# High and low f16 parts, scaled by powers of two, in the output projection of a hybrid attention block

## The chip, the cores and the metric

The kernel runs on one core of a Trainium2 chip. The metric is the device time of one execution in microseconds (us), and beside it stands a profile of one execution, taken by the hardware profiler. The engines are named as in the profile: PE does matrix products (PEld is its weight load), DVE is the vector engine, ACT the scalar engine, POOL is GpSimd, and SP issues nearly all transfers. Each engine works through its own instructions in order and waits for others by semaphores.

## The reference

One encoder layer on x of 1024 tokens by 1024 channels, all in float32:

```python
h = x @ W_in                                  # split by columns into q, k, v, z of two groups
y_a = neighborhood_attention(q_a, k_a, v_a, rel_bias)   # 8 heads of 64, window 8 x 16 on a 16 x 64 grid
y_b = windowed_gqa_with_sink(rotary(q_b), rotary(k_b), v_b, sink)   # 8 query heads, 2 key/value heads, |i-j| <= 128
mixed = concat([y_a * silu(z_a), y_b * silu(z_b)], axis=-1)         # (1024, 1024)
y = mixed @ W_out                             # (1024, 1024)
x = layer_norm(2 ** 0.25 * x + y, gain, bias)
```

The kernel computes `mixed` transposed, in eight tiles of 128 channels by 1024 tokens. Channel tile e holds two heads: e = 0 to 3 are group a, e = 4 to 7 are group b.

## The kernel before

**Precision.** A float32 product is made of three products of shorter parts: high by high, high by low, and low by high, where high is the value rounded to the short type and low the rest. The input projections use f16 parts. They are scaled by powers of two which are found on chip, so that the parts stay in the range of f16, and later steps take the scale out again (`w_scale`, `w_split`). The output projection uses fp32r parts, a float32 form that PE takes at a shorter precision; the profile prints it as f32. It needs no scale.

**Stages.** A first stage, up to about 62 us, loads x and computes v. Then come the projections of `ORDER` (21 column tiles of 128), six of them alone, and the other 15 as *fill* between the attention steps. The attention stage has 128 units: 64 of group b and then 64 of group a, one of 128 queries each. For unit i PE computes scores into a bank of PSUM (`stage_qk`, two products; there are four such banks, tag "s"), DVE adds the bias and finds the row's bound (L719), ACT takes the exponential (L735) and the high part of the probabilities (L745), DVE takes the low part (L746), and SP sends them through a transposing transfer (L749). Six to nine steps later PE multiplies them by v (`stage_pv`, L774), DVE divides by the sum (L783), and PE turns each finished pair of heads round (L794). DVE then multiplies by the gate z and a factor from `z_col` (L797, L803): this is m = `mixed` transposed, kept in the tile of z.

**What sets the order of the work.** The attention stage is written out by hand. The main loop runs over steps i. At a step, PE gets the scores of unit i and then a share of fill (`pump_to`, after the times in `FILL_AT`). Other work waits in four queues ("act", "dve", "pool", "sp") and is let out by `pop` at fixed places, a few operations a step; `need` forces out what something later depends on. The output projection stands at the end of the fill: `out_head` multiplies the channel tiles e = 4 to 7, which are ready first, for some token tiles while attention still runs. `final` does the rest; there, up to the last token tile, the framework's scheduler orders the instructions of each engine.

**The output projection.** `WO_SEQ` numbers the 16 half tiles of w_out (128 by 512, one e and one half a of the output columns): n = 0 to 7 are e = 4 to 7, first for a = 0 and then for a = 1; n = 8 to 15 are e = 0 to 3. `wo_load` loads one at step `WO_LD[n]`. `wo_split` makes its two parts: it copies to the high part (L860, on ACT or DVE) and subtracts for the low part (L864, DVE where n % 3 is 2, else POOL). n = 0 to 7 are split at the steps of `WO_AT` and n = 8 to 15 in `final`. The loads of n = 14 and 15 wait for the splits of 4 and 5. `m_queue` and `m_split` do the same with m: copies on ACT (L880, L831), subtractions on POOL (L881) and DVE (L832). `out_mms` issues the three products for one token tile t, half a and e (L899). All products of one (t, a) add up in a PSUM bank, and `residual` (L946) adds 2 ** 0.25 times x to it on DVE, which also takes the sums for the layer norm. `norm` and `norm_last` do the rest with ACT, DVE and POOL. x_load fetches the tiles of x again for the residual; six tiles fit, so those of t = 6 and 7 are loaded when 0 and 1 have been stored.

The three products of the output projection:

```python
for i, (lh, rh) in enumerate(((mh[e], woh), (mh[e], wol), (ml[e], woh))):
    nc.tensor.matmul(ps, lh[:, ts], rh[:, cs],
                     start=(e == EO[0] and i == 0), stop=(e == EO[-1] and i == 2))
```

Of the kernel before, what the change touches and what calls it, by code (L numbers as in the profile page):

```python
# [24 lines left out]
PSCALE = 2.0 ** 14  # L25
QSCALE = 2.0 ** -15
# [29 lines left out]
def hybrid_block(ctx, tc, xT, x, wt, wv, wo, bias, sink, gain, lbias, cos, sin, bmask, out):  # L56
# [42 lines left out]
    vscb = const.tile([128, 2], F32, name="vscb")  # L99
# [104 lines left out]
    def w_scale(n):  # L204
        g, v = wg[:, n:n + 1], inv[:, n:n + 1]
        c, m = (2 * n, 2) if n < NPRO else (2 * NPRO, NS)
        ps = bank("t")
        nc.tensor.matmul(ps[:, :m], ones, wm.bitcast(BF16)[:, 2 * c + 1:2 * (c + m):2], start=True, stop=True)
        nc.vector.tensor_reduce(g, ps[:, :m], axis=mybir.AxisListType.X, op=ALU.add if n < NPRO else ALU.max)
        nc.vector.tensor_scalar_max(g, g, 2.0 ** -30)  # L210
        nc.vector.tensor_scalar(g.bitcast(I32), g.bitcast(I32), 0x7F800000, None, op0=ALU.bitwise_and)
        nc.vector.tensor_scalar(wsc[:, n:n + 1].bitcast(I32), g.bitcast(I32), 0x7F800000, None, op0=ALU.bitwise_xor)
# [112 lines left out]
    def z_col(e):  # L325
        return vsc if e in (4, 0, 5) else vscb[:, 0:1] if e == 1 else vscb[:, 1:2]
# [496 lines left out]
    def m_alloc(e, pool):  # L823
        for parts_ in (mh, ml):
            if pool is big:
                parts_[e] = big_tile(f"m{e}", (128, S))
            else:
                parts_[e] = pool.tile([128, S], F32R, tag="m", name=f"m{e}", bufs=8)

    def m_split(e, sl, hi, lo):  # L830
        hi(mh[e][:, sl], zt[e][:, sl])  # L831
        lo(ml[e][:, sl], zt[e][:, sl], mh[e][:, sl].bitcast(F32))  # L832
# [6 lines left out]
    def wo_load(n):  # L839
        if n < 16:  # L840
            tag = WO_TAG[n]
            pool, bufs = (rawp, 3) if tag == "raw" else (wp, {"wr": 5, "wor": 2}[tag])
            raw = pool.tile([128, 512], F32, tag=tag, name=f"wor{n}", bufs=bufs)
            e, a = WO_SEQ[n]
            nc.sync.dma_start(raw, wo[e, :, 512 * a:512 * a + 512])
            wo_raw[n] = raw

    wo_ops = {}

    def wo_split(n):  # L850
        def hi():
            if n < 8:
                t = big_tile(f"wo{n}")
            elif n < 13:
                t = tiles["fp"].tile([128, 2, 512], F32R, tag="wo", name=f"wo{n}", bufs=5)
            else:
                t = zp.tile([128, 2, 512], F32R, tag=("zc", "zd", "ze")[n - 13], name=f"wo{n}", bufs=1)
            wo_parts[n] = [t[:, 0, :], t[:, 1, :]]
            copy = nc.scalar.copy if hi_eng == "act" else nc.vector.tensor_copy
            copy(wo_parts[n][0], wo_raw[n])  # L860

        def lo():
            h, l = wo_parts[n]
            eng.tensor_sub(l, wo_raw.pop(n), h.bitcast(F32))  # L864

        eng, q = (nc.vector, "dve") if n % 3 == 2 else (nc.gpsimd, "pool")
# [4 lines left out]
        if 4 <= n < 6:  # L871
            load_ops["wo", n + 10] = enq("sp", lambda: wo_load(n + 10), o)
# [3 lines left out]
    def m_queue(e):  # L876
        m_alloc(e, big)
        m_ops[e] = []
        for h in (slice(0, 512), slice(512, S)):
            o = enq("act", lambda h=h: nc.scalar.copy(mh[e][:, h], zt[e][:, h]))  # L880
            m_ops[e].append(enq("pool", lambda h=h: nc.gpsimd.tensor_sub(  # L881
                ml[e][:, h], zt[e][:, h], mh[e][:, h].bitcast(F32)), o))
# [33 lines left out]
    def final():  # L916
# [5 lines left out]
        for e in EO[4:]:  # L922
            m_alloc(e, fp)
# [10 lines left out]
        def x_load(t):  # L934
            if t < 8:
                xrs[t] = fp.tile([128, D], F32, tag="xr", name="xr", bufs=NX)
                nc.sync.dma_start(xrs[t], x[t])

        def residual(t, a, ps, c=None):
            if a == 0:  # L940
                stats[t] = fp.tile([128, 4, 6], F32, tag="stats", name="stats")
            for k in range(2) if t == 7 and c is None else (c,):
# [3 lines left out]
                nc.vector.scalar_tensor_tensor(xv, xv, ALPHA, ps[:, o:o + w], op0=ALU.mult, op1=ALU.add)  # L946
# [91 lines left out]
    for i in range(-LD, NU + LO):  # L1038
# [9 lines left out]
        for n in range(len(WO_LD)):  # L1048
# [123 lines left out]
```

## Time and profile before

| what | us |
|---|---|
| median of 3 runs | 455.44 (455.09 to 457.77) |
| the profiled execution | 455.45 |
| its span, first to last instruction | 453.7 |
| PE busy | 443.1 |
| DVE busy | 333.9 |
| ACT busy | 288.0 |
| POOL busy | 228.1 |
| mean granted clock of PE, as a share of full speed | 0.994 |

The profiled execution's own time is 1.75 us longer than its span, since the span begins with the first instruction and ends with the last. "Busy" is the time in which an engine has an instruction running. Matmuls overlap each other in the records, so a mean duration of one (379 ns) isn't the pace at which they follow each other; the pace is read from the chain of work that ended last, whose pieces don't overlap. A row of the groups reads: line, engine, operation, what it writes and reads with partitions and elements, count, then busy time and mean duration of one, then the engine's idle time ahead of it and what ended that. A row of the chain reads: start, length, what.

### The profile page before, as it was taken

What the parts mean: (1) busy time and instruction counts of PE and PEld (TensorE: products, weight loads), DVE (VectorE), ACT (ScalarE), POOL (GpSimd) and SP (SyncE); (2) the same over time, 40 slices, a digit from 0 to 9 for tenths busy, and PEclk for the clock granted to TensorE, in tenths of its full rate; (3) what the DMA queues carried; (4) which work ended last, traced back from release to release, by engine and by line L of the source; (5) the groups of instructions that cost most, each with busy time, mean ns of one, the idle gap of its engine ahead of it and who ended that gap; (6) DMA issues with size and microseconds to landing.
All of it is one profiled execution on the core that took longest, in us unless ns stands there. A gap on an engine that the chain in (4) does not pass through costs nothing.

```text
span 453.7 us, 9395 instructions
## 1 busy us (share of the span) xinstructions
PE 443.1 (98%) x3239; PEld 293.1 (65%) x3239; DVE 333.9 (74%) x808; ACT 288.0 (63%) x664; POOL 228.1 (50%) x235
## 2 busy tenths in 40 slices
PE   8999999999999999999999999999999999999993
PEld 6999974444445565555555656555556788888883
DVE  5885956538987777896888878877878739099644
ACT  5648649776489877788778887686878824012100
POOL 0003944546948559688326766446663444007621
PEclk9999999999999999999999999999999999999997
DMA  7897278984557796687889779999989877004511
GB/s 249 291 320 266 76 247 259 309 307 177 208 103 167 151 176 152 112 176 139 167 154 174 174 161 216 190 175 232 188 166 225 165 230 286 0 17 147 187 54 61
DMA packets 134415, 82.28 MB, mean 181 GB/s; under 512 B 101344, under 2 KB 113504, under 8 KB 134112
## 3 DMA queue, kind: packets, MB, share of 16 engines
q1 hardware_dynamic: 134224, 81.61, 72.3%
q8 instruction: 25, 0.41, 0.4%
q14 instruction: 22, 0.18, 0.2%
q10 hardware_dynamic: 144, 0.08, 0.1%
HBM read 51.25 MB, written 9.96 MB: 135 GB/s over the span
## 4 chain that ended last, share of the span: by engine, by line
PE 91%; DVE 3%; issue 2%; ACT 2%; DMA 1%; SPq 0%; DVEq 0%; ACTq 0%
PE ps_pj L356 44%; PE ps_s L899 9%; PE ps_t L774 6%; PE ps_s L430 6%; PE ps_pj L899 6%; PE ps_t L899 5%; PE ps_s L709 4%; PE ps_s L710 4%; PE ps_pj L430 3%; PE ps_t L430 3%; PE ps_t L794 1%; DVE qs L241 1%; DMA wvraw<-in_wv 1%; ACT split L745 1%; DVE split L746 1%
## 5 line engine op out<-in xcount | busy, mean ns | idle before, releaser
L356 PE MATMUL ps_pj<-xf,wh 128*128 128x512 f16 x672 | 202.1, 379 | 0.9 <-DVE qs L241 0.6
L356 PE MATMUL ps_pj<-xf,wl 128*128 128x512 f16 x336 | 127.3, 379 | 0.0
L356 PEld LDWEIGHTS <-wh 128*128 128x128 f16 x672 | 63.5, 98 | 61.6 <-DVE ks L241 1.1
L735 ACT ACTIVATE ps_s<-sn,nm 128x385 f32<-128x385 f32 (+3 forms) x128 | 70.3, 549 | 32.8 <-DVE nm L719 31.7
L746 DVE SCALAR_TENSOR_TENSOR split<-ps_s,split 128x384 f16<-128x384 f32 (+2 forms) x128 | 65.7, 513 | 27.7 <-ACT split L745 26.3
L745 ACT ACTIVATE split<-ps_s 128x384 f16<-128x384 f32 (+2 forms) x128 | 57.6, 450 | 1.8
L356 PEld LDWEIGHTS <-wl 128*128 128x128 f16 x336 | 32.9, 98 | 37.4
L719 DVE CUSTOM_DVE_ANT_0 sn<-ps_s,bm,nsk 128x384 f32<-128x384 f32 (+1 forms) x64 | 40.8, 638 | 6.8 <-PE ps_s L710 6.2
L899 PE MATMUL ps_s<-wo,m 128*128 128x512 f32 (+1 forms) x192 | 43.3, 379 | 0.0
L719 DVE CUSTOM_DVE_ANT_0 sn<-ps_s,bias,sg 128x264 f32<-128x264 f32 (+1 forms) x64 | 35.0, 548 | 10.9 <-PE ps_s L710 4.7
L187 POOL TENSOR_SCALAR wr<-wr,wsc 128x512 f32<-128x512 f32 x26 | 20.7, 796 | 39.8 <-ACT wh L182 33.7
L709 PE MATMUL ps_s<-ks,qs 128*128 128x384 f16 (+4 forms) x128 | 39.3, 307 | 0.0
L710 PE MATMUL ps_s<-ks,qs 128*128 128x384 f16 (+4 forms) x128 | 39.2, 306 | 0.0
L899 PEld LDWEIGHTS ps_s<-wo,m 128*128 128x128 f32 x192 | 34.4, 188 | 7.0
L774 PEld LDWEIGHTS <-tr 128*128 128x128 f16 (+1 forms) x1104 | 36.5, 98 | 2.2 <-issue 0.3
L681 POOL TENSOR_SCALAR bias<-bias,rsg 128x552 f32<-128x552 f32 (+1 forms) x24 | 19.3, 802 | 36.4 <-DMA bias<-in_bias 25.5
L953 ACT ACTIVATE sd<-mv,eps 128x1 f32<-128x1 f32 x8 | 2.4, 295 | 50.5 <-DVE mv L951 46.5
L188 POOL TENSOR_TENSOR wl<-wr,wh 128x512 f16<-128x512 f32 x26 | 32.6, 1256 | 2.2
L273 POOL COPY ks<-ks 64x512 f16<-64x512 f16 x40 | 26.4, 666 | 10.9 <-DVE ks L241 6.1
L989 POOL TENSOR_TENSOR xr<-xr,gb 128x512 f32<-128x512 f32 x7 | 10.3, 1474 | 40.8 <-ACT xr L986 40.8
L430 PE MATMUL ps_s<-wvh,x 128*128 128x320 f32 x128 | 29.5, 310 | 0.0
L899 PE MATMUL ps_pj<-wo,m 128*128 128x512 f32 (+1 forms) x120 | 28.7, 377 | 0.0
(147 smaller groups left out, 825.6 us busy)
## 6 DMA issues: line engine op xcount, KB each, us to landing
xraw<-in_xT SPq DMA_DIRECT2D x31, 256.0 KB, 4.3
ws<-in_wt SPq DMA_DIRECT2D x15, 512.0 KB, 5.2
wr<-in_wt SPq DMA_DIRECT2D x26, 256.0 KB, 3.0
bias<-in_bias SPq DMA_DIRECT2D x16, 276.0 KB, 3.4
wor<-in_wo SPq DMA_DIRECT2D x16, 256.0 KB, 3.2
xr<-in_x SPq DMA_DIRECT2D x8, 512.0 KB, 7.3
out<-xr SPq DMA_DIRECT2D x14, 256.0 KB, 2.1
bias<-in_bias SPq DMA_DIRECT2D x8, 368.0 KB, 3.9
```

The lines of the kernel that those rows point to most:

```text
L188: nc.gpsimd.tensor_sub(l, raw, h)
L273: nc.gpsimd.tensor_copy(t[o, sl], t[a, sl])
L356: nc.tensor.matmul(ps, a[:, k % 4, :], mv, start=(k == 0 and i == 0), stop=(k == KT - 1 and i == 2))
L430: nc.tensor.matmul(ps[:, :320], lh[t // 4, k][:, ts], rh[k][:, cs], start=(k == 0 and i == 0), stop=(k == KT - 1 and i == 2))
L709: nc.tensor.matmul(ps[:, :m], q, sl[0], start=True, stop=False)
L710: nc.tensor.matmul(ps[:, :m], q, sl[1], start=False, stop=True)
L719: nc.vector.tensor_tensor_reduce(sn[:, :m], ps[:, :m], bias_t, sg[:, c:c + 1], init, op0=ALU.add, op1=ALU.min, accum_out=nm)
L735: nc.scalar.activation(pt[:, :m], sn[:, :m], AF.Exp, bias=nm, scale=-1.0, accum_out=sm[:, k:k + 1])
L745: nc.scalar.activation(hl[:, :m, 0, :c], src, AF.Copy, scale=PSCALE)
L746: nc.vector.scalar_tensor_tensor(hl[:, :m, 1, :c], src, PSCALE, hl[:, :m, 0, :c], op0=ALU.mult, op1=ALU.subtract)
L774: nc.tensor.matmul(ps[:, HD * m:HD * m + HD], a, b_, start=(i == 0), stop=(i == len(mms) - 1))
L899: nc.tensor.matmul(ps, lh[:, ts], rh[:, cs], start=(e == EO[0] and i == 0), stop=(e == EO[-1] and i == 2))
```

## The change

The parts of m and of w_out become f16 tiles; high and low part of one tensor share a tile, and two halves of w_out share one. For the range:

- `z_col` gives factors divided by the largest of the weight scales and multiplied by 2 ** -44, made in `w_scale` by six small DVE operations in place of two (`zc`, `zi`, `mc`). So m comes out in the range of f16 without an operation of its own.
- w_out is multiplied by a power of two, `wos`, from the largest of 16 sums of absolute values. Ten half tiles are summed on DVE after their usual load (n = 0 to 8 and 11). Six (`WO_SCAN`: 9, 12, 10, 13, 14, 15) are loaded an extra time at steps 2 to 13 and summed on ACT, in place. At step 55 `wo_scale` adds up the partitions by one small matmul and makes `wos` and `yc` by five small DVE operations.
- `wo_split` multiplies by `wos`: the high part still in one operation; the low part in one on DVE and in two on POOL. DVE has the low parts of n = 2, 5, 8, 9, 10, 11 and 14. The splits of n = 4 to 7 move from steps 128 to 131 to steps 84, 88, 93 and 98.
- The scale goes out in `residual`: the product is multiplied by `yc`, and 2 ** 0.25 times x is made ahead by ACT after each load of x.

```diff
+MSCALE = 2.0 ** -44
+WO_SCAN = ((9, 2), (12, 4), (10, 6), (13, 8), (14, 10), (15, 13))
+WO_PREV = {15: ("s", 9), 0: ("s", 10), 1: ("s", 15), 2: ("s", 12), 3: ("s", 13), 11: ("s", 14)}
+WO_SCALE = 55
-WO_AT = [67, 71, 75, 79, 128, 129, 130, 131]
-WO_LD = [18, 22, 26, 30, 36, 39, 42, 45, 48, 112, 116, 33, 130, 130]
+WO_AT = [67, 71, 75, 79, 84, 88, 93, 98]
+WO_LD = [16, 22, 19, 25, 36, 39, 42, 45, 48, 112, 116, 28, 130, 130, 130, 130]
...
-            nc.vector.tensor_scalar(vscb[:, i:i + 1], v, vsc, 0.5, op0=ALU.mult, op1=ALU.mult)
...
+            nc.vector.tensor_reduce(zi[:, 0:1], inv, axis=mybir.AxisListType.X, op=ALU.max)
+            nc.vector.reciprocal(zi[:, 1:2], zi[:, 0:1])
+            nc.vector.tensor_scalar_mul(zc[:, 0:1], zi[:, 1:2], MSCALE)
+            for i, a in ((1, NPRO - 1), (2, NPRO)):
+                nc.vector.tensor_scalar(zc[:, i:i + 1], inv[:, a:a + 1], zi[:, 1:2], 0.5 * MSCALE, op0=ALU.mult, op1=ALU.mult)
+            nc.vector.tensor_scalar(mc, zi[:, 0:1], vsc, 0.5 / MSCALE, op0=ALU.mult, op1=ALU.mult)
...
     def z_col(e):
-        return vsc if e in (4, 0, 5) else vscb[:, 0:1] if e == 1 else vscb[:, 1:2]
+        i = 0 if e in (4, 0, 5) else 1 if e == 1 else 2
+        return zc[:, i:i + 1]
...
+    def m_alloc(e):
+        if e >= 4:
+            t = big_tile(f"m{e}", (128, 2, S), F16)
+        else:
+            t = tiles["fp"].tile([128, 2, S], F16, tag="m", name=f"m{e}", bufs=4)
+        mh[e], ml[e] = t[:, 0, :], t[:, 1, :]
...
+    def wo_scan(n, scan=False):
+        def act():
+            raw = wo_raw.pop(("s", n))
+            nc.scalar.activation(raw, raw, AF.Abs, accum_out=wom[:, n:n + 1])
+
+        def dve():
+            nc.vector.tensor_reduce(wom[:, n:n + 1], wo_raw[n], axis=mybir.AxisListType.X, op=ALU.add,
+                                    apply_absolute_value=True)
+
+        load = load_ops["wo", ("s", n) if scan else n]
+        wo_ops["s", n] = enq("act", act, load) if scan else enq("dve", dve, load)
+
+    def wo_scale():
+        need(*[wo_ops["s", n] for n in range(16)])
+        ps = bank("t")
+        nc.tensor.matmul(ps[:, :16], ones, wom.bitcast(BF16)[:, 1::2], start=True, stop=True)
+        nc.vector.tensor_reduce(wog, ps[:, :16], axis=mybir.AxisListType.X, op=ALU.max)
+        nc.vector.tensor_scalar_max(wog, wog, 2.0 ** -30)
+        nc.vector.tensor_scalar(wog.bitcast(I32), wog.bitcast(I32), 0x7F800000, None, op0=ALU.bitwise_and)
+        nc.vector.tensor_scalar(wos.bitcast(I32), wog.bitcast(I32), 0x7F800000, None, op0=ALU.bitwise_xor)
+        nc.vector.tensor_scalar(yc, wog, mc, 1.0, op0=ALU.mult, op1=ALU.mult)
...
     def wo_split(n):
         def hi():
...
-            copy = nc.scalar.copy if hi_eng == "act" else nc.vector.tensor_copy
-            copy(wo_parts[n][0], wo_raw[n])
+            if hi_eng == "act":
+                nc.scalar.activation(wo_parts[n][0], wo_raw[n], AF.Copy, scale=wos)
+            else:
+                nc.vector.tensor_scalar_mul(wo_parts[n][0], wo_raw[n], wos)
 
         def lo():
             h, l = wo_parts[n]
-            eng.tensor_sub(l, wo_raw.pop(n), h.bitcast(F32))
-
-        eng, q = (nc.vector, "dve") if n % 3 == 2 else (nc.gpsimd, "pool")
+            raw = wo_raw.pop(n)
+            if q == "dve":
+                nc.vector.scalar_tensor_tensor(l, raw, wos, h, op0=ALU.mult, op1=ALU.subtract)
+            else:
+                nc.gpsimd.tensor_scalar(raw, raw, wos, 1.0, op0=ALU.mult, op1=ALU.mult)
+                nc.gpsimd.tensor_sub(l, raw, h)
+
+        q = "dve" if n in (2, 5, 8, 9, 10, 11, 14) else "pool"
...
-        if 4 <= n < 6:
-            load_ops["wo", n + 10] = enq("sp", lambda: wo_load(n + 10), o)
...
                 nc.sync.dma_start(xrs[t], x[t])
+                nc.scalar.activation(xrs[t], xrs[t], AF.Copy, scale=ALPHA)
...
-                nc.vector.scalar_tensor_tensor(xv, xv, ALPHA, ps[:, o:o + w], op0=ALU.mult, op1=ALU.add)
+                nc.vector.scalar_tensor_tensor(xv, ps[:, o:o + w], yc, xv, op0=ALU.mult, op1=ALU.add)
...
+        for n, at_ in WO_SCAN:
+            if at_ == i:
+                load_ops["wo", ("s", n)] = enq("sp", lambda n=n: wo_load(n, True), wo_ops.get(WO_PREV.get(n) if n == 15 else None))
+                wo_scan(n, True)
+        for n in range(16):
             if WO_LD[n] == i:
-                load_ops["wo", n] = enq("sp", lambda n=n: wo_load(n), wo_ops.get({9: 0, 10: 1, 12: 2, 13: 3}.get(n)),
+                load_ops["wo", n] = enq("sp", lambda n=n: wo_load(n), wo_ops.get(WO_PREV.get(n) if n < 15 else None),
+                                        wo_ops.get({9: 0, 10: 1, 12: 2, 13: 3, 14: 4, 15: 5}.get(n)),
                                         w_ops.get(17 + n if 4 <= n <= 8 else None))
+                if n < 9 or n == 11:
+                    wo_scan(n)
+        if i == WO_SCALE:
+            wo_scale()
```

More of the change, by code (lines that the diff above doesn't have):

```diff
@@ L821, in hybrid_block @@
     EO = (4, 5, 6, 7, 0, 1, 2, 3)
[L823 to L828, printed above, removed]
+    def m_alloc(e):
[4 more added lines that the diff above has]
+        mh[e], ml[e] = t[:, 0, :], t[:, 1, :]
     def m_split(e, sl, hi, lo):
         hi(mh[e][:, sl], zt[e][:, sl])
[L832 removed]
+        lo(ml[e][:, sl], zt[e][:, sl], mh[e][:, sl])
     WO_SEQ = [(e, a) for a in range(2) for e in EO[:4]] + [(e, a) for e in EO[4:] for a in range(2)]
@@ L837, in hybrid_block, with wo_load @@
     wo_raw = {}
[L839 to L846, printed above, removed]
-    wo_ops = {}
+    def wo_load(n, scan=False):
+        tag = ("wor" if n in (9, 10, 15) else "raw") if scan else WO_TAG[n]
+        pool, bufs = (rawp, 3) if tag == "raw" else (wp, {"wr": 5, "wor": 2}[tag])
+        raw = pool.tile([128, 512], F32, tag=tag, name=f"wor{n}", bufs=bufs)
+        e, a = WO_SEQ[n]
+        nc.sync.dma_start(raw, wo[e, :, 512 * a:512 * a + 512])
+        wo_raw[("s", n) if scan else n] = raw
```

27 lines of the change are left out of this document (16 added, 11 removed).

## The prediction

> **What bounds the kernel now.** I read the page first, then the waits of PE, then the chain that ended last in order of time.
>
> ```profile
> span 453.7 us, 9395 instructions
> PE 443.1 (98%) x3239; PEld 293.1 (65%) x3239; DVE 333.9 (74%) x808; ACT 288.0 (63%) x664; POOL 228.1 (50%) x235
> ...
> PE 91%; DVE 3%; issue 2%; ACT 2%; DMA 1%; SPq 0%; DVEq 0%; ACTq 0%
> ```
>
> A busy PE alone proves little, because matmul ends are modelled. The last line says more: the work that ended last was PE work for 91% of the span. The waits of PE, all of them, are these:
>
> ```profile
> PE ps_t L390 <- DVE warm L387: 1.3, 1, 1.3
> PE ps_pj L430 <- ACT wvh L414: 0.7, 1, 0.7
> PE ps_pj L356 <- DVE qs L241: 0.6, 1, 0.6
> PE ps_pj L356 <- DVE ks L241: 0.4, 1, 0.4
> ```
>
> That is 3.0 us in the whole kernel, and none of it in the output projection (L899). So a microsecond taken from a matmul's pace should come off the end, as long as the other engines still deliver in time. The second condition is where the risk lies.
>
> **The matmuls of the output projection.** The chain gives their pace, beside that of f16 matmuls of the same 128x512 shape (L356), each of which loads weights of its own too:
>
> ```profile
> 81.67 10.38 PE ps_pj L356 x48
> ...
> 359.84 2.75 PE ps_s L899 x12
> ...
> 401.70 5.53 PE ps_pj L899 x24
> ...
> 443.17 2.87 PE ps_pj L899 x24
> ```
>
> f16: 10.38 / 48 = 0.216 us. fp32r (which the trace prints as f32): 5.53 / 24 = 0.230, or 2.75 / 12 = 0.229 in the gentler place. The last row is the 256-wide form: 2.87 / 24 = 0.120, against half of 0.216 = 0.108, my estimate for f16, since no f16 row has that width.
>
> ```profile
> L899 PE MATMUL ps_s<-wo,m 128*128 128x512 f32 (+1 forms) x192 | 43.3, 379 | 0.0
> L899 PE MATMUL ps_pj<-wo,m 128*128 128x512 f32 (+1 forms) x120 | 28.7, 377 | 0.0
> L899 PE MATMUL ps_t<-wo,m 128*128 128x512 f32 x96 | 24.0, 393 | 0.0
> ```
>
> 192 + 120 + 96 = 408 matmuls: 8 token tiles x 8 e x 3 products, 360 at 512 wide and 48 at 256 wide. The products stay three, so the count stays. Saved: 360 x (0.230 - 0.216) = 5.1, and 48 x 0.012 = 0.6, together **5.7 us**. By the gentler pace it is 360 x 0.013 + 0.6 = 5.3. The upper bound comes from the chain's shares by line:
>
> ```profile
> by line: PE ps_pj L356 44.3%; PE ps_s L899 9.2%; PE ps_t L774 6.5%; PE ps_s L430 6.2%; PE ps_pj L899 5.6%; PE ps_t L899 4.9%; PE ps_s L709 3.6%; PE ps_s L710 3.6%; PE ps_pj L430 3.1%; PE ps_t L430 3.1%; issue 1.8%; PE ps_t L794 1.4%; DVE qs
> ```
>
> 9.2 + 5.6 + 4.9 = 19.7% of 453.7 is 89.4 us. At f16 pace it would be 360 x 0.216 + 48 x 0.108 = 82.9, so 6.5 saved. I take 5.7, the plain count.
>
> **What is added for it.** The sums of |w_out| need all 16 half tiles before the first split. Ten are scanned where they already land (DVE, one reduction each); six are loaded twice, and their first copy is scanned on ACT.
>
> ```profile
> L202 ACT ACTIVATE junk<-wr 128x512 bf16<-128x512 f32 x12 | 7.6, 632 | 0.2
> L202 ACT ACTIVATION_READ_ACCUMULATOR junk<-wr 128x1 f32 x12 | 2.3, 194 | 0.0
> L439 DVE TENSOR_REDUCE xm<-x 128x1 f32<-128x512 f32 x16 | 9.8, 680 | 0.0
> L212 DVE TENSOR_SCALAR wsc<-wg 128x1 int32<-128x1 int32 x7 | 1.1, 153 | 0.2
> ```
>
> ACT: 6 x (0.63 + 0.19) = 4.9 us. DVE: 10 x 0.68 = 6.8 us, plus five scalar operations at step 55 and five more on balance where the weight scale is made: 10 x 0.153 = 1.5 us. All of it lies in the attention stage or just ahead of it:
>
> ```profile
> 122.00:200.00 78.00, 78.00 (x654) 43.75 (x653) 62.79 (x179) 61.83 (x157) 52.82 (x53) 1.00 0.72 145
> ```
>
> (After PE and PEld come DVE, ACT, POOL.) DVE is busy 80% here and ACT 79%, and PE all the time. On average the additions fit: 16 us are idle on ACT in these 78. Locally they don't quite. In the changed program's order, ACT scans stand at about units 5, 10 (two), 11, 15 and 20, so four of them, 3.3 us, fall into 12 us in which ACT has 12 x 21% = 2.5 us free; and DVE enters 0.8 us later from its five constants. ACT then runs 1.6 (0.8 + 3.3 - 2.5) to 4.1 us (no idle time usable) behind its old times. What does PE allow? A score bank is free again when DVE has split that unit, and PE needs it four units on:
>
> ```profile
> 148.89 0.55 DVE L746 SCALAR_TENSOR_TENSOR split<-ps_s,split 128x384 f16<-128x384 f32 x1
> ...
> 151.98 0.33 PE L709 MATMUL ps_s<-ks,qs 128*128 128x384 f16 x1
> ```
>
> This is one of the tightest pairs (unit 13 and unit 17): 151.98 - 149.44 = 2.5 us of slack. So the loss is 0 to 4.1 - 2.5 = 1.6 us; I take **0.4**, nearer the end at which ACT's idle time is usable, as it mostly waits for DVE there.
>
> The six extra loads go into SP's queue, in front of transposes:
>
> ```profile
> L845 SPq DMA_DIRECT2D wor<-in_wo x16: 376/554/996, 155.9 to 367.6; - x16
> ...
> DMA to landing us min/median/max: 3.0/3.2/5.1
> ```
> ```profile
> 136.01 6.49 SPq L749 DMA_TRANSPOSE tr<-split  x5
> ```
>
> A transpose holds SP 6.49 / 5 = 1.3 us and a load 0.55; 128 units lie between about 122 and 359.84 us (the row above), 1.86 each. Five extra loads lie in the first 14 units, so SP slips by up to 5 x 0.55 = 2.8 us, less its idle time. Five first loads (w_out 0, 2, 3, 11 and, unmoved, 1) now stand at steps 16 to 28 instead of 18 to 33, among the same transposes. PV comes some five units after a unit's transpose, which covers this; I cost it at nothing, and give the case without cover below.
>
> The 128x16 matmul of the sums waits for the last DVE scan. In the program's order that scan is two units earlier, and the bank it writes was emptied before; behind the matmul stand the scores of unit 55 and all fill. Cost: 0 to 1 us (one DVE unit of lag), taken at **0.1**.
>
> **The splits.** They change form, and those of w_out 4 to 7 move from steps 128-131 to 84-98, out of the crowded end.
>
> ```profile
> L182 ACT ACTIVATE wh<-wr,wsc 128x512 f16<-128x512 f32 x26 | 18.5, 711 | 0.2
> L860 ACT CAST wo<-wor 128x512 fp32r<-128x512 f32 x12 | 7.0, 613 | 8.3 <-DMA wor<-in_wo 8.3
> L187 POOL TENSOR_SCALAR wr<-wr,wsc 128x512 f32<-128x512 f32 x26 | 20.7, 796 | 39.8 <-ACT wh L182 33.7 <-PE ps_s L710 3.7 <-PE ps_t L774 2.1
> L188 POOL TENSOR_TENSOR wl<-wr,wh 128x512 f16<-128x512 f32 x26 | 32.6, 1256 | 2.2
> L864 POOL TENSOR_TENSOR wo<-wor,wo 128x512 fp32r<-128x512 f32 x11 | 15.4, 1417 | 16.5 <-ACT wo L860 15.7 <-DMA xr<-in_x 0.8
> L481 DVE SCALAR_TENSOR_TENSOR xf<-xraw,xsc,xf 128x512 f16<-128x512 f32 x11 | 11.8, 1112 | 1.3 <-ACT xf L476 1.3
> ```
>
> High part on ACT: +0.1 us each. Low part on POOL: 0.80 + 1.26 = 2.06 against 1.42. On DVE 1.11. In the attention stage this is 6 x 0.64 = 3.9 us more on POOL, which is idle a third of the time; nothing. It matters at the hand-over to the second half, e = 0 to 3, whose splits can't begin before the last attention output:
>
> ```profile
> 373.98 5.50 PE ps_t L899 x24
> ```
> ```profile
> 374.82 1.19 DVE L860 CAST wo<-wor 128x512 fp32r<-128x512 f32 x3
> 375.94 3.49 DVE L832 TENSOR_TENSOR m<-z,m 128x512 fp32r<-128x512 f32 x2
> 379.34 2.38 DVE L864 TENSOR_TENSOR wo<-wor,wo 128x512 fp32r<-128x512 f32 x2
> 381.65 3.69 DVE L832 TENSOR_TENSOR m<-z,m 128x512 fp32r<-128x512 f32 x6
> ```
> ```profile
> 375.81 4.76 POOL L864 TENSOR_TENSOR wo<-wor,wo 128x512 fp32r<-128x512 f32 x3 [0.75 <-DMA xr<-in_x]
> ```
>
> PE has 24 matmuls in hand from 373.98: 24 x 0.216 = 5.2 us, and then 24 per e. DVE subtractions took 1.75 us each beside POOL (3.49 / 2) and 0.62 without (3.69 / 6). From 374.8 DVE now does four high parts, 0.4 (1.19 / 3) to 0.7 us each, and then eight subtractions until e = 0 and 1 are whole. POOL works 3 x 2.06 = 6.2 us here, which is as long as 6.2 / 1.75, some four subtractions: 1.6 to 2.8, plus 8 x 0.62 = 5.0 to 4 x 1.75 + 4 x 0.62 = 9.5, is 6.6 to 12.3 us. By the new order of PE the last of the eight is wanted some 31 matmuls into e = 0 and 1, at 373.98 + 5.2 + 6.7 = 385.9, 11.1 us on. Loss 0 to 1.2; or, if DVE and POOL hold each other up throughout, 2.8 + 8 x 1.75 = 16.8, 5.7 late. I take **0.4**, near the lower end, where today's PE has lost next to nothing. Here the Trainium skill speaks against the change: "SBUF — State Buffer", section "Who interferes with whom", says that a DVE instruction with two SBUF inputs and a GpSimd instruction that reads SBUF exclude each other for a whole instruction. The trace agrees (1.75 beside POOL, 0.62 alone); by that rule alone each of the eight would meet a POOL instruction while POOL has any, and the sum would be 455.45 - 5.7 + 0.5 + 1.2 = 451.5.
>
> **The tail.** The residual keeps its one DVE instruction (its factor moves from x to the product). ACT scales each residual tile by alpha ahead of time, 128x1024:
>
> ```profile
> L595 ACT ACTIVATE junk<-ws 128x1024 bf16<-128x1024 f32 x12 | 12.6, 1048 | 0.1
> ```
>
> 8 x 1.05 = 8.4 us on an ACT that is nearly idle there. For tiles 6 and 7 it waits for their loads, and square roots of earlier rows queue behind it, and DVE behind those; PE has a free bank for each group left, so this is caught up before tile 7. The stretch after the last matmul is the same set of operations. It begins here, so it is 453.7 - 446.04 = 7.7 us, before and after:
>
> ```profile
> 446.04 0.02 issue
> ```
>
> **The sum.** The profiled execution took 455.45 us for a span of 453.7 (1.75 around it); the median of the runs is 455.44. 455.45 - 5.7 + 0.4 + 0.1 + 0.4 = 450.65; I say **450.6 us**.
>
> **The rivals.** (1) *Attention starves.* The scans push DVE past the 2.5 us everywhere, not once: 1.6 us lost early and another 1 to 2 during the ten DVE scans (steps 16 to 50). For: 80% busy. Against: no PE wait in this stage today. 455.45 - 5.7 + 3 + 0.5 = 453.3. (2) *The hand-over stalls* by 1.2 to 5.7, say 3 us: 455.45 - 5.7 + 0.5 + 3 = 453.3. For: the 1.75 us rows. Against: w_out 4 to 7 are off POOL by then. (3) *Slower: ACT waits for its scans' loads.* A scan stands on ACT ahead of a unit's split; if its load has not landed, ACT, DVE's split, and SP's next transposes stop, and the next scan's load stands behind those transposes. Each such wait is 0.55 + 3.2 = 3.75 us. It decides once SP is more than about 3.5 us behind, since the loads are issued some 7 us ahead. Three to five waits less the slack of 2.5 are 8.8 to 16.3 us: with the gain, 458.6 to 466.1, taken at 461. Against: SP catches up today. (4) *f16 doesn't run at 0.216 here*, because these matmuls alternate banks and operands: nothing saved, losses kept, 455.5 to 457. Against: the L356 row, with a weight load for each matmul.
>
> **How the numbers follow.** Forecast 0.60 (its own range 449.0 to 451.6: gain 5.3 to 6.5, losses 0 to 1.5), rivals (1) 0.13, (2) 0.10, (3) 0.11, (4) 0.06. One per cent, about what a measurement tells from no change, is 4.55 us: faster needs 450.9 or less. That is five sixths of the forecast, 0.50; slower over 460 is most of (3), 0.09; the rest is 0.41. The range 449.0 to 456.0 leaves out (3) and the ends of (4) and the forecast, under 0.2.
>
> **What would show it.** Right: L899's successors print f16, 24 of them in 5.2 us in the steady part; PE waits stay near 3 us; the fill's end comes at most 0.5 us later than 359.8. Wrong: new PE waits for "split" or "tr" between 135 and 215 us (rival 1, or 3 if ACT waits for "wor"), PE waiting for wo or m between 378 and 392 (rival 2), or a pace of 0.23 (rival 4).

## The result and the profile after

| | before | changed |
|---|---|---|
| median of the runs, us | 455.84 (455.09 to 457.77, 6 runs) | 451.68 (450.62 to 453.04, 6 runs) |
| the profiled execution | 455.45 | 451.44 |
| its span | 453.7 | 449.6 |

The ratio is 0.9905, with a 95% interval of 0.9885 to 0.9926: the changed kernel is about 4.2 us faster, where 4.8 were forecast. The page of the changed kernel, in the lines that answer to those of before (span, busy time by engine, the chain's shares):

```profile
span 449.6 us, 9438 instructions
...
PE 438.1 (97%) x3240; PEld 260.8 (58%) x3240; DVE 341.7 (76%) x829; ACT 300.2 (67%) x684; POOL 230.4 (51%) x242
...
PE 78%; DVE 10%; ACT 5%; issue 4%; DMA 2%; SPq 0%; DVEq 0%; ACTq 0%
```

PE's share of the chain fell from 91% to 78%, and DVE's rose from 3% to 10%: other engines now decide for longer what comes next. The waits of PE in the changed kernel, all that the view lists (total, times, longest):

```profile
PE ps_t L406 <- DVE warm L403: 1.3, 1, 1.3
PE ps_pj L372 <- DVE ks L256: 1.1, 3, 0.7
PE ps_pj L372 <- DVE qs L256: 0.6, 1, 0.6
PE ps_t L790 <- DMA tr<-split: 0.4, 1, 0.4
PE ps_t L446 <- DVE x L414: 0.2, 1, 0.2
```

L372 is the projections' matmul (L356 before), L256 the low part of k and q (L241 before), L790 is PV (L774 before). One wait for k's low part has become three, and one for a transpose is new. The time is best split by PE's own stations. First the projections' first matmul, before (L356) and in the changed kernel (L372), from the two timelines:

```profile
61.93 0.61 PE L356 MATMUL ps_pj<-xf,wh 128*128 128x512 f16 x2
```
```profile
61.85 0.61 PE L372 MATMUL ps_pj<-xf,wh 128*128 128x512 f16 x2
```

Then the output projection (L899 before, L941 now) in the two chains, from its first product to its last group:

```profile
351.27 0.78 PE ps_pj L899 x3
```
```profile
353.11 0.65 PE ps_pj L941 x3
...
400.30 5.18 PE ps_pj L941 x24
...
439.18 2.63 PE ps_pj L941 x24
```

- From the first projection to the first product of the output projection: 353.11 - 61.85 = 291.26 us, before 351.27 - 61.93 = 289.34. **1.92 us lost.**
- From there to the end of the last matmul: 439.18 + 2.63 - 353.11 = 88.70, before 446.04 - 351.27 = 94.77. **6.07 won.** The pace is 5.18 / 24 = 0.216 us at 512 wide and 2.63 / 24 = 0.110 at 256 wide.
- The tail: 449.6 - 441.81 = 7.79, before 7.66. 0.13 lost.

So the gain came as it was worked out, and a third of it was given back ahead of the place where it is made. Below, kernels are compared by the **stretch** from the first projection's matmul to the end of the span: before 453.7 - 61.93 = 391.77, changed 449.6 - 61.85 = 387.75. The stage ahead of it is the same code in all of them, but ended at 61.7 to 64.2 us.

Where the 1.9 us went is in the chain of the changed kernel. Some of its pieces in the attention stage, those by which the reading goes:

```profile
168.34 3.36 DMA wor<-in_wo
...
172.33 0.67 DVE sn L735
...
177.48 0.67 DVE wom L871
...
181.39 0.68 DVE ks L256
...
183.83 0.69 DVE ks L256
...
189.61 0.68 DVE ks L256
...
192.05 0.70 DVE ks L256
192.79 1.46 PE ps_pj L372 x6
...
246.50 1.47 PE ps_pj L372 x6
```

A load of w_out, a sum on DVE (L871), the low parts of k (L256), and then PE: the projection's bank is free for the next group only when DVE has taken k's low part out of it. Compared unit by unit with before, PE's scores fall behind by 0.28 us at unit 14, 0.92 at unit 34, 0.32 at unit 38 and 0.38 at unit 67, and otherwise by next to nothing until the f16 products begin.

### The profile page after: what moved, and what is told of

Its sections match the earlier page's. It is cut to its first block, busy times and chain, and to the rows that moved or that the text cites. A ratio compares the mean times of both kernels' runs of the same rounds, so it can differ in the third digit from the quotient of the medians.

```text
span 449.6 us, 9438 instructions
## 1 busy us (share of the span) xinstructions
PE 438.1 (97%) x3240; PEld 260.8 (58%) x3240; DVE 341.7 (76%) x829; ACT 300.2 (67%) x684; POOL 230.4 (51%) x242
## 4 chain that ended last, share of the span: by engine, by line
PE 78%; DVE 10%; ACT 5%; issue 4%; DMA 2%; SPq 0%; DVEq 0%; ACTq 0%
PE ps_pj L372 34%; PE ps_s L941 9%; PE ps_s L446 6%; PE ps_t L790 5%; PE ps_pj L941 5%; PE ps_t L941 5%; PE ps_pj L446 3%; PE ps_t L446 3%; PE ps_s L725 3%; PE ps_s L726 3%; ACT split L761 2%; PE ps_t L810 1%; ACT ps_s L751 1%; DVE sn L735 1%; DVE ks L256 1%
## 5 line engine op out<-in xcount | busy, mean ns | idle before, releaser
L372 PE MATMUL ps_pj<-xf,wh 128*128 128x512 f16 x672 | 202.2, 379 | 1.7 <-DVE ks L256 1.1
L372 PE MATMUL ps_pj<-xf,wl 128*128 128x512 f16 x336 | 127.3, 379 | 0.0
L372 PEld LDWEIGHTS <-wh 128*128 128x128 f16 x672 | 63.5, 98 | 62.6 <-DVE ks L256 1.7
L941 PEld LDWEIGHTS <-m 128*128 128x128 f16 x408 | 39.6, 98 | 41.3 <-DVE m L848 0.2
L372 PEld LDWEIGHTS <-wl 128*128 128x128 f16 x336 | 32.8, 98 | 37.4
L735 DVE CUSTOM_DVE_ANT_0 sn<-ps_s,bias,sg 128x264 f32<-128x264 f32 (+1 forms) x64 | 35.0, 547 | 9.9 <-PE ps_s L726 2.7
L735 DVE CUSTOM_DVE_ANT_0 sn<-ps_s,bm,nsk 128x384 f32<-128x384 f32 (+1 forms) x64 | 40.7, 636 | 0.4 <-PE ps_s L726 0.3
L941 PE MATMUL ps_s<-wo,m 128*128 128x512 f16 (+1 forms) x192 | 40.8, 366 | 0.0
L790 PEld LDWEIGHTS <-tr 128*128 128x128 f16 (+1 forms) x1104 | 36.7, 98 | 2.9 <-DMA tr<-split 0.7
L941 PE MATMUL ps_pj<-wo,m 128*128 128x512 f16 (+1 forms) x120 | 26.1, 358 | 0.0
```

Source lines behind the costliest of these rows:

```text
L372: nc.tensor.matmul(ps, a[:, k % 4, :], mv, start=(k == 0 and i == 0), stop=(k == KT - 1 and i == 2))
L735: nc.vector.tensor_tensor_reduce(sn[:, :m], ps[:, :m], bias_t, sg[:, c:c + 1], init, op0=ALU.add, op1=ALU.min, accum_out=nm)
L790: nc.tensor.matmul(ps[:, HD * m:HD * m + HD], a, b_, start=(i == 0), stop=(i == len(mms) - 1))
L941: nc.tensor.matmul(ps, lh[:, ts], rh[:, cs], start=(e == EO[0] and i == 0), stop=(e == EO[-1] and i == 2))
```

## The experiments

The table has all of them. "Attention" is the time from PE's scores of unit 0 to those of unit 121. A ratio goes by the kernel before as it ran in the same set, where its medians were 455.84 to 456.94. Stretch and attention are those of one profiled execution each.

| kernel | median, us | ratio to before (95%) | stretch | attention |
|---|---|---|---|---|
| before | 455.84 | 1 | 391.77 | 225.03 |
| changed | 451.68 | 0.9905 (0.9885 to 0.9926) | 387.75 | 226.96 |
| changed, again | 451.39 | 0.9882 (0.9864 to 0.9900) | 387.08 | 226.03 |
| no sums | 450.10 | 0.9865 (0.9845 to 0.9886) | 385.80 | 225.12 |
| extra loads only | 450.98 | 0.9884 (0.9863 to 0.9906) | 385.89 | 225.11 |
| DVE's sums only | 449.51 | 0.9850 (0.9828 to 0.9872) | 385.82 | 225.20 |
| ACT's sums only | 452.12 | 0.9911 (0.9895 to 0.9928) | 388.50 | 225.24 |
| ACT's sums only, again | 450.52 | 0.9865 (0.9842 to 0.9888) | 386.03 | 225.19 |
| before, with all sums | 457.48 | 1.0032 (1.0016 to 1.0047) | 393.15 | 226.26 |
| DVE's sums one step sooner | 455.07 | 0.9972 (0.9955 to 0.9990) | 391.06 | 229.79 |
| splits of 4 to 7 late | 451.39 | 0.9908 (0.9888 to 0.9928) | 387.55 | 226.52 |
| ACT's sums ahead of attention | 450.84 | 0.9881 (0.9863 to 0.9900) | 386.41 | 225.24 |
| the same, two loads earlier | 449.89 | 0.9848 (0.9830 to 0.9866) | 386.09 | 225.23 |

### The sums taken apart

Without any sums:

```diff
+    nc.vector.memset(wom, 2.0)
...
-        need(*[wo_ops["s", n] for n in range(16)])
+        need()
...
-        for n, at_ in WO_SCAN:
+        for n, at_ in ():
...
-                if n < 9 or n == 11:
-                    wo_scan(n)
```

> The changed kernel without the sums of |w_out|: no extra loads, no scans on ACT, none on DVE. The sums tile is filled with a constant, so that the weight scale is a fixed power of two; all else (f16 parts, scale matmul, splits, residual) stays. Theory: the 1.84 us that the output projection starts later in the changed kernel come from the sums. Then all of it goes: the first product of the steady output projection at 351.3 and not 353.1, time 451.7 - 1.8 = 449.9. Rival: the lateness comes from the rest (the six small operations of the weight scales, the new order of the loads, the first splits from unit 67 on); then 451.7, first product at 353.1. Rival (4) of the prediction is out already by the pace.

The stretch is 385.80, 1.95 us less than in the changed kernel, and attention takes 225.12, as before. PE waits once for k's low part, as in the old kernel, and for no transpose:

```profile
PE ps_pj L373 <- DVE ks L257: 0.4, 1, 0.4
```

So in these profiles the sums are the whole loss, and without them the change wins 391.77 - 385.80 = 5.97 us. The extra loads only:

```diff
+    nc.vector.memset(wom, 2.0)
...
-                wo_scan(n, True)
+                wo_ops["s", n] = load_ops["wo", ("s", n)]
...
-                if n < 9 or n == 11:
-                    wo_scan(n)
```

> The changed kernel with the six extra loads in SP's queue, but nothing summed (no scans on ACT or DVE; the sums tile is filled with a constant). Theory A, the scans on DVE keep the low parts of k, and with them the projection's bank, waiting: the loads cost only the 0.28 us at unit 14, where PV waited for a transpose; 449.9 + 0.3 = 450.2. Rival B, the loads push the transposes back and all else follows from it: at least 1.5 of the 1.84 us stay, 451.4 to 451.7.

The stretch is 385.89, 0.1 us over the kernel without sums: by it both theories were too high, and the loads by themselves cost nothing in this execution. The medians, 450.98 and 450.10, differ by 0.9 us with intervals that overlap, so the other executions leave a small cost open. DVE's ten sums only (no extra loads, nothing on ACT):

```diff
+    nc.vector.memset(wom, 2.0)
...
-        for n, at_ in WO_SCAN:
+        for n, at_ in ():
```

> The changed kernel with the ten sums on DVE, but without the six extra loads and their sums on ACT (their columns of the sums tile hold a constant). Theory A: the loss from unit 34 on stays (0.92 + 0.32 + 0.38 = 1.6 us), 451.3 to 451.5, with PE waiting for ks L256 there. Rival B: 449.9 to 450.2. Rival C, ACT's six sums are what makes ACT and then DVE late for good: also 449.9 to 450.2, but then the second run of this set (loads alone) is at 450 too.

385.82. My theory A falls: the loss from unit 34 on doesn't come from DVE's sums alone. The kernel before, with all the sums added and their result used nowhere:

```diff
+                wo_scan(n, True)
...
+                if n < 9 or n == 11:
+                    wo_scan(n)
+        if i == WO_SCALE:
+            wo_scale()
```

> The kernel before, with fp32r parts as they were, and the sums added to it: the six extra loads with their scans on ACT, the ten scans on DVE, the new order of the first loads, the scale matmul and its five small operations. The scale is made and used nowhere. Theory: the loss belongs to the sums and not to f16, so that the kernel before gets slower by it, 455.8 + 1.8 = 457.6. Rival: the loss belongs to the other edits; then 455.8. Together with the changed kernel this also gives the gain of f16 without the loss: 457.6 - 451.7 = 5.9 by the theory, 4.1 by the rival.

393.15, that is 1.38 us slower in the stretch and 1.4 in the median (interval 0.16 to 0.47%), with losses at the same units 34, 38 and 67 (0.48, 0.32 and 0.33 us). The loss belongs to the sums, whatever the output projection does. ACT's six sums only (extra loads kept, DVE's ten left out), twice:

```diff
+    nc.vector.memset(wom, 2.0)
...
-                if n < 9 or n == 11:
-                    wo_scan(n)
```

> The changed kernel with the six extra loads and their sums on ACT, but without the ten sums on DVE (their columns of the sums tile hold a constant). Loads alone and DVE sums alone cost PE 0 and 0.17 us by the start of its scores. Theory: a lag with thresholds. ACT's sums push DVE behind PE; the lag is 0.8 us at unit 22 and 1.5 from unit 24 on, where the first DVE sums stand; PE pays what goes beyond 0.6 us at unit 34, beyond 0.25 at unit 38 and all that is left at unit 67. Then without the DVE sums the lag at unit 32 is about 0.8, and the loss is 0.3 (unit 14) + 0.2 (unit 34) + at most 0.2 later = 0.5 to 0.7, time 450.1 + 0.6 = 450.7. Rival: costs add up, the ACT sums cost all but the DVE sums' 0.17; loss 1.7, 451.7.

> The changed kernel with ACT's six sums but without DVE's ten, a second time. The first time it lost 0.2 us in attention up to unit 121, but 2.5 us at 347 to 365, where PE waited for transposes behind a slow load of w_out. Theory: a chance of that execution; now 386.0 to 386.5 from the first matmul of the projections to the end, 450.3 us. Rival: it belongs to this order of instructions and comes again, 388 to 389, 452.1 us, as the median of the first set says.

In attention the loss was 0.1 us both times: less than either theory, and far from the 1.7 of costs that add up. 0.1 + 0.1 for the parts is not the 0.9 to 1.8 of the whole. The first of the two executions lost 2.5 us later, which the second did not; there one load of w_out held SP for 2.56 us instead of the 0.58 of the load before it, and PE then waited 1.8 us for transposes (timeline of SP):

```profile
345.38 2.56 SPq L861 DMA_DIRECT2D wor<-in_wo  x1
```

The two medians, 452.12 and 450.52, differ as the two profiles do, and five of the six times of the first set lie above 451.7, so more than one execution was slow. Why that load was slow, and whether it was in the others too, stays open.

### What the lag does

Take DVE's lag as the time from PE's scores of a unit to DVE's work on them (L735; L736 where lines are shifted by one). For unit 32, in the changed kernel and in the one without sums, with PE's scores of units 33 and 34 behind it (timelines of PE and of DVE):

```profile
180.87 0.27 PE L725 MATMUL ps_s<-ks,qs 128*128 128x256 f16 x1
...
182.38 0.33 PE L725 MATMUL ps_s<-ks,qs 128*128 128x384 f16 x1
...
183.95 0.43 PE L790 MATMUL ps_t<-vb,tr 128*128 128x64 f16 x9 [0.38 <-DMA tr<-split]
184.58 0.60 PE L372 MATMUL ps_pj<-xf,wh 128*128 128x512 f16 x2 [0.20 <-DVE ks L256]
...
185.89 0.33 PE L725 MATMUL ps_s<-ks,qs 128*128 128x384 f16 x1
```
```profile
184.74 0.54 DVE L735 CUSTOM_DVE_ANT_0 sn<-ps_s,bm,nsk 128x256 f32<-128x256 f32 x1
```
```profile
180.45 0.27 PE L726 MATMUL ps_s<-ks,qs 128*128 128x256 f16 x1
...
181.96 0.33 PE L726 MATMUL ps_s<-ks,qs 128*128 128x384 f16 x1
...
184.54 0.33 PE L726 MATMUL ps_s<-ks,qs 128*128 128x384 f16 x1
```
```profile
182.81 0.54 DVE L736 CUSTOM_DVE_ANT_0 sn<-ps_s,bm,nsk 128x256 f32<-128x256 f32 x1
```

The lag is 184.74 - 180.87 = 3.87 us against 182.81 - 180.45 = 2.36: DVE is 1.51 us later than it would be. From unit 33 to unit 34 PE takes 3.51 us against 2.58: 0.93 lost. The new wait for a transpose lies in this stretch too, but the one for k's low part ends behind it, so k's low part sets the time. The same two numbers, always less those of the kernel without sums, for three places:

```
                         unit 32 -> 34   unit 36 -> 38   unit 66 -> 67     DVE's third sum
                          lag    loss     lag    loss     lag    loss      waited for its load
changed                  1.51    0.93     0.58   0.32     0.31   0.31      1.12
splits of 4 to 7 late    1.26    0.68     0.59   0.32     0.35   0.35      0.54
before, with all sums    1.07    0.48     0.59   0.32     0.33   0.33      0.59
changed, again           0.81    0.22     0.59   0.33     0.36   0.35      0
ACT's sums only          0.29    0.11     0.19   0        0      0         -
ACT's sums only, again   0.28    0        0.29   0.02     0.05   0.04      -
DVE's sums only          0.01    0        0.01   0        0.08   0.08      0
```

The pattern is a threshold at each place: PE pays the lag less 0.59 us at unit 34, less 0.27 at unit 38, and all of it at unit 67. One number doesn't follow, the 0.11 of the first run with ACT's sums only: there PV's 33 matmuls took 1.23 us instead of 1.12, which is not the wait for k's low part.

As lags the parts do add up: at unit 20 it is 2.12 us with ACT's sums alone, 0.58 with DVE's alone, and 2.71 with both (changed, again). The lag is used up only where DVE has time to spare. Between units 24 and 26 it has some: there the lag falls from 1.38 to 0 with ACT's sums alone, and by 1.40, from 2.05 to 0.65, in the second execution of the changed kernel. In its first execution it falls only from 1.70 to 1.51, and is still 1.5 at unit 32. So the loss is what is left of the lag over the thresholds, and that is why the parts cost 0.1 and the whole 0.9 to 1.8.

The last column names a second cause. DVE's third sum stands between units 24 and 26. In the first execution it found its load missing, all of DVE stood behind it, and the 1.12 us were taken from the time in which DVE would have caught up. The load was late rather than slow: it landed 3.36 us after its issue, but, counted from the first projection, it was issued 1.70 us later than in the second execution (168.34 - 61.85 against 167.51 - 62.72, from SP's timelines). To test it, DVE's sums were let out one step sooner after their loads were put in SP's queue, and nothing else was moved:

```diff
+        if not scan:
+            load.lag = 1
```

> The changed kernel with DVE's sums let out one step sooner after their loads: three of the four that stand ahead of unit 32 move forward by one unit in DVE's order (after scores of units 21, 24, 27, where they were after 22, 25, 28). Nothing else is moved. In the executions so far with both kinds of sums, the third of them waited 1.12, 0.59, 0.54, 0 and 0.44 us for its load, and PE lost 0.92, 0.47, 0.67, 0.22 and 0 us at unit 34. Theory: DVE stands still behind a load that the transposes hold back on SP, and this is what lifts the lag over the threshold. One unit sooner makes the wait longer by up to 1.8 us, so that the third sum waits 1.5 to 3 us, and PE loses 1.3 to 3 us by unit 38 (changed kernel: 1.25 and 0.56 in two executions); from the first matmul of the projections to the end 388 to 389.5. Rival: the wait is chance of a slow load and has nothing to do with the place; then the waits stay at 0 to 1.1 and the stretch at 387.1 to 387.8.

The third sum in the changed kernel, and the second and third in this one (timelines of DVE, with the idle time ahead of them and what ended it):

```profile
171.73 0.69 DVE L871 TENSOR_REDUCE wom<-wor 128x1 f32<-128x512 f32 x1 [1.12 <-DMA wor<-in_wo]
```
```profile
164.67 0.69 DVE L871 TENSOR_REDUCE wom<-wor 128x1 f32<-128x512 f32 x1 [0.52 <-DMA wor<-in_wo]
...
171.18 0.69 DVE L871 TENSOR_REDUCE wom<-wor 128x1 f32<-128x512 f32 x1 [1.62 <-DMA wor<-in_wo]
```

DVE waits 2.1 us in all, its lag at unit 32 is 2.98 us over that of the kernel without sums, and PE loses 3.25 us from unit 33 to unit 34. The median is 455.07: three sums moved forward by one unit cost 3 to 4 us (ratio 0.9972 against 0.9905 and 0.9882), most of what the whole change wins. The direction is that of the theory, the size is more. The threshold gives 2.98 - 0.59 = 2.4, and the rest is PE's clock, which costs another 0.75 us from unit 34 to unit 35. Ahead of that PE lost 0.7 us in all at units 28, 29, 32 and 33, where it waited for a score bank (its scores began 0.05 us after DVE's split of four units earlier): with a lag of up to 3.9 us their slack of 2.5 didn't hold. The wait of PE, and its matmuls after it (timeline), then the busy times of two microseconds each around it (the third figure from the end is the granted clock):

```profile
186.47 0.74 PE L372 MATMUL ps_pj<-xf,wh 128*128 128x512 f16 x2 [2.15 <-DVE ks L256]
...
187.43 1.06 PE L372 MATMUL ps_pj<-xf,wh 128*128 128x512 f16 x2
188.28 0.63 PE L372 MATMUL ps_pj<-xf,wl 128*128 128x512 f16 x1
```
```profile
184.00:186.00 2.00, 0.33 (x12) 0.20 (x7) 1.26 (x4) 1.98 (x6) 1.88 (x4) 1.00 0.51 98
186.00:188.00 2.00, 1.53 (x5) 0.65 (x6) 1.94 (x6) 1.13 (x5) 1.86 (x3) 0.70 0.52 98
188.00:190.00 2.00, 2.00 (x7) 0.74 (x6) 1.60 (x6) 1.95 (x6) 1.62 (x2) 0.50 0.34 66
```

From 187.43 to 188.28 two matmuls take 0.85 us, 0.43 each instead of 0.216; the full pace is back from about 190.2.

### The changed kernel again

> The changed kernel itself, beside the other two of this set, so that they have a comparison on one chip. Theory: PE loses 0.9 and 0.3 us at units 34 and 38 and 0.4 at unit 67 again, as these come from the order of instructions; the 0.28 at unit 14 was chance and need not come again. The stretch from the first matmul of the projections to the end is 387.4 to 387.8. Rival: all of these are chance, and the stretch comes out between 386 and 389.

387.08. The losses at units 38 and 67 are the same to 0.05 us. That at unit 34 is 0.22 instead of 0.93, as this time no load was late for DVE, and the 0.28 at unit 14 is gone. So neither theory was wholly right: two of the four losses belong to the order of instructions, one to chance, and one to both. With 451.39 beside 456.94 of before, the ratio is 0.9882.

### The splits of w_out 4 to 7

```diff
-WO_AT = [67, 71, 75, 79, 84, 88, 93, 98]
+WO_AT = [67, 71, 75, 79, 128, 129, 130, 131]
```

> The changed kernel with the splits of w_out 4 to 7 back at steps 128 to 131, from 84, 88, 93 and 98. The prediction held against a stall at the hand-over that these splits are off POOL by then. If that is the reason, then with 3 x 2.06 = 6.2 us of POOL work more (5 is on DVE), 4 x 0.71 us on ACT and the loads of 12 to 15 later, PE waits for wo or m between 350 and 392 us for 1 to 4 us: 452.7 to 455.7. Rival: DVE sets the hand-over, and POOL and the loads have room: 451.7, PE's waits in the output projection stay at 0.2 us.

387.55, between the two executions of the changed kernel, and the output projection's weight loads wait 0.2 us for m, as in the changed kernel. POOL and the loads have room there; my reason against a stall at the hand-over wasn't what prevents it.

### A version that beats both

ACT's sums go where ACT waited for PE, ahead of the attention stage:

```diff
-WO_SCAN = ((9, 2), (12, 4), (10, 6), (13, 8), (14, 10), (15, 13))
+WO_SCAN = ((9, 190, 228), (12, 192, 230), (10, 194, 232), (13, 196, 234), (14, 198, 262), (15, 242, 280))
...
+    for n, c0, c1 in WO_SCAN:
+        events.setdefault(c0, []).append(lambda n=n: early_load(n))
+        events.setdefault(c1, []).append(lambda n=n: early_scan(n))
```

> The changed kernel with the six extra loads and ACT's sums moved ahead of the attention stage: loads at 190 to 198 and 242 of the 288 matmuls of the first projections, sums at 228 to 234, 262 and 280, where ACT waited for PE for 3.5, 1.5 and 2.4 us between 110 and 125 us. Nothing is left out. Theory: the lag never arises; DVE's ten sums alone cost 0.17 us; 449.6 to 450.0, first product of the steady output projection near 351.4. Rival: the loads collide with the loads of v and weights there, or ACT's sums delay the copies that the projections' bank waits for, and PE loses at 108 to 125 what it gains later: 451 to 452.

386.41, 0.7 to 1.3 us less than the changed kernel, and 0.1 us lost in attention. Another 0.14 went at 352 us and 0.22 at 364 us, where PV waited for transposes. With w_out 9 and 10 loaded at steps 80 and 84 as well:

```diff
-WO_LD = [16, 22, 19, 25, 36, 39, 42, 45, 48, 112, 116, 28, 130, 130, 130, 130]
+WO_LD = [16, 22, 19, 25, 36, 39, 42, 45, 48, 80, 84, 28, 130, 130, 130, 130]
```

> The changed kernel with ACT's sums ahead of the attention stage as in the run before, and the second loads of w_out 9 and 10 at steps 80 and 84 in place of 112 and 116. Nothing is left out. From the first matmul of the projections to the end of the span the changed kernel took 387.75 us, the one without sums 385.80, the one with the early sums 386.41: of its 0.6 us too many, 0.2 is the wait for ks L256 at unit 67, and 0.4 the wait for a transpose at 363 us, after a load of w_out and one of the bias had been slow at 344 to 350. Theory: the w_out loads crowd that place; with them gone the stretch is 386.0, time about 450.0 where the changed kernel has 451.7. Rival: that wait was chance, and the stretch stays at 386.0 to 386.5.

386.09 and 449.89 us, ratio 0.9848 (0.9830 to 0.9866), beside 0.9882 (0.9864 to 0.9900) for the changed kernel of the same set. Four of the five times are 449.69 to 450.07, where the changed kernel took 451.26 to 451.56; the fifth is the profiled execution, 451.87, whose first stage ended late, at 64.0 us. The stretch is 0.3 over that of the kernel without sums. Whether the two loads did it or the earlier wait was chance, one profile of each can't say. In its timeline of ACT the sums (L835) lie ahead of the attention stage, up to the last, which comes late:

```profile
112.82 0.63 ACT L835 ACTIVATE wor<-wor 128x512 f32<-128x512 f32 x1
...
116.26 0.60 ACT L304 ACTIVATE rp_raw<-ps_pj 128x512 f32<-128x512 f32 x1 [0.45 <-PE ps_pj L372]
...
127.57 0.63 ACT L835 ACTIVATE wor<-wor 128x512 f32<-128x512 f32 x1 [3.29 <-DMA wor<-in_wo]
```

ACT still waits 0.45 us for PE at 116.26, so the first four cost nothing. The sixth waits 3.29 us for its load; DVE is 1 us late in units 0 to 12 for it. With DVE's own sums the lag is still 1.6 us at unit 20, but it is gone at unit 26, ahead of every threshold.

## Why the prediction was right, and where it was wrong

The forecast was 450.6, the median is 451.68, inside the range and 0.1 us above the forecast's own range. That the number came so near is in part luck: the losses, 1.92 + 0.13 = 2.0 us in the profiled execution, lie outside the 0 to 1.5 of that range, and a gain above the count made up for some of it. Of the prediction's own signs, the pace came out, but the fill ended 1.2 us later than before and not at most 0.5 (chain, against 359.84 before):

```profile
361.06 2.59 PE ps_s L941 x12
```

By the steps of the prediction:

- **The gain, 5.7 us (5.3 to 6.5): right.** 5.97 by the kernel without sums, 6.07 by the stretch of the output projection. The 256-wide estimate, 0.108 us, measured 0.110. By the count it is 360 x (5.53 - 5.18) / 24 + 48 x (2.87 - 2.63) / 24 = 5.7; the rest lies in small gaps of the old projection, where eleven products were followed by the next only after 0.31 to 0.36 us (starts in PE's timeline). The count of 408 is right, though 8 token tiles x 8 e x 3 leaves out the two halves of the output columns.
- **Attention's scans, 0.4 (0 to 1.6): mis-sized, and the step that failed.** The mechanism was half right. The lag was set at 1.6 to 4.1 us and was 2.4 at unit 20, as DVE had it from ACT; the slack of the score banks, 2.5, held, and PE lost nothing for want of one. (Of that lag 0.8 us was to be DVE's later start; DVE's first scores came 2.18 us behind PE's against 1.84, so it was 0.34.) But I compared the lag with one bank at one place, and took it for gone afterwards ("on average the additions fit"). It lasted, less what DVE made up at units 24 to 26, for a dozen units and met another bank, the projection's, with 0.59, 0.27 and 0 us of slack. Loss: 1.84 in the profiled execution and 0.91 in a second one.
- **Six extra loads at nothing, since PV covers them: right for the loads alone (0.1 in the stretch), wrong in company.** I looked for the cover of the transposes and not for that of DVE, whose own sums stand behind the same queue. DVE waited 1.12 us in one execution and not at all in another.
- **The wait of the scale's matmul, 0.1:** 0.03 at unit 55.
- **The hand-over, 0.4 (0 to 5.7):** at most 0.2, all that PE's weight loads waited for m (L848). Eight operations of DVE were to take 5.0 to 9.5 us and took 384.96 - 376.83 = 8.1. DVE and POOL in the changed kernel (their timelines):

```profile
376.83 0.68 DVE L848 TENSOR_TENSOR m<-z,m 128x512 f16<-128x512 f32 x1
377.43 3.32 DVE L905 SCALAR_TENSOR_TENSOR wo<-wor,wos,wo 128x512 f16<-128x512 f32 x3
380.67 1.70 DVE L848 TENSOR_TENSOR m<-z,m 128x512 f16<-128x512 f32 x2
382.29 2.74 DVE L905 SCALAR_TENSOR_TENSOR wo<-wor,wos,wo 128x512 f16<-128x512 f32 x2
384.96 4.05 DVE L848 TENSOR_TENSOR m<-z,m 128x512 f16<-128x512 f32 x5
```
```profile
376.61 2.04 POOL L907 TENSOR_SCALAR wor<-wor,wos 128x512 f32<-128x512 f32 x1 [20.45 <-DMA xr<-in_x]
```

  DVE's two-input operations take 0.68 to 1.37 us each here, none of them the 1.75 of before, and POOL's first multiplication took 2.04 us, and the next two 1.37 each, instead of the 0.80 I had: this time POOL was slowed more than DVE. The Trainium skill, "SBUF — State Buffer", section "Who interferes with whom", says that the issue order decides who blocks. That would fit, but no run here changed the order. The 451.5 us that I gave by that page came near the result for another reason: the hand-over didn't cost its 1.2 us.
- **The tail, nothing:** 0.13 us.

Of the rivals, (1) is what happened in kind, attention starving, at half its price or less and by another bank, and its sign, a new wait for a transpose, stands at 183.95 us; (3) did happen, but on DVE instead of ACT, and the run with the sums one step sooner shows how near it was: one step more and the kernel is at 455. (2) and (4) didn't occur.

## What to carry to other kernels

A lag that an engine picks up in a tight stage stays with it until it has idle time in its own order, and is paid at the narrowest place behind, not where it arose; so look for the smallest slack among all banks and buffers that the engine frees from there on. Costs of parts tried alone don't add up then, and a part that costs nothing alone may be half of the loss in company. An instruction that has time, such as a sum needed much later, belongs where its engine waits anyway, and far enough behind its load that it can't stop the engine.

## What the runs showed of the hardware that was not expected

- In the run with the sums one step sooner, a wait of 2.15 us was followed by half of PE's clock (granted 0.50, matmuls at 0.43 us) for some 3 us, so that this stall of PE cost more than its length. Waits of 0.7 us, as at 246.5 us in the changed kernel, left it at 1.00. Where between the two the limit lies, no run shows. The Trainium skill, "TensorE: Matmul & The Clock Gate", section "What's actually happening", puts the drop behind at least one idle window of about 3.4 us; by that rule this wait would have been harmless, and here it was not.
- In f16 a weight load of the output projection takes 98 ns, in fp32r 188 (the groups of weight loads, changed and before). The pace can't be read from that: at 256 wide the fp32r matmuls, each with a weight load of its own, follow each other at 0.120 us, in less time than one load takes. Why the pace at 512 wide is 0.230 and not 0.216 us, no run shows.

```profile
L941 PEld LDWEIGHTS <-m 128*128 128x128 f16 x408 | 39.6, 98 | 41.3 <-DVE m L848 0.2
```
```profile
L899 PEld LDWEIGHTS ps_s<-wo,m 128*128 128x128 f32 x192 | 34.4, 188 | 7.0
```

- The time from the first projection to the first scores was 62.40 or 62.41 us in each of the profiled executions, while the stage ahead, which loads x and the weights of v, ended between 61.7 and 64.2. In these profiles that stage alone spreads as widely as the runs of one kernel do, which is why small differences were read from stretches here.
